# One VectorE transpose a level in a triangular inverse, the spreading and the constant terms given to other engines

## The chip, the cores and the metric

The kernel runs on one core of a Trainium2 chip. The core has five engines that run beside each other and wait for one another by semaphores: TensorE (PE, its weight loads PEld), VectorE (DVE), ScalarE (ACT), GpSimd (POOL) and SyncE (SP), whose queue issues the DMA transfers here. Each engine takes its own instructions in order. The metric is the device time of one execution in microseconds (us), lower is better; a kernel's time is the median of its runs.

## The reference

A two-layer trunk over 256 context and 1024 latent tokens of width 1024. In each layer a normalised and modulated input is projected once; half of the columns feed a retention group, the other half an RWKV-7 group of 8 heads of 64, in both directions of time. The part that matters here is the RWKV-7 scan, a generalised delta rule over a state of 64x64 a head:

```
S_t = S_{t-1} diag(w_t) - (S_{t-1} kap_t)(kap_t*a_t)^T + v_t k_t^T
y_t = S_t r_t
decay = exp(-exp(-softplus(-(w0 + tanh(xw) @ w2)) - 0.5))
```

With `decay = exp(-exp(-0.5) * sigmoid(z))` and `sigmoid(z) = 0.5*(1 + tanh(z/2))`, the product of decays over a stretch of tokens is an exponential of a running sum of `1 + tanh`.

## The kernel before

The scan is done in chunks of 64 tokens. A stage is one head pair (128 channels, two heads), two chunks, both directions: 10 stages a head pair, 4 head pairs a layer, 2 layers, so 80 stages. Three functions make a stage.

`prep` (L893 to L932) loads the features of a stage into `ft` (single-buffered), sums `1 + tanh` over each chunk of 64 with four VectorE scans (L908, L909; the `+ 1` of the first channel set, index 0, is the `ones` operand of the scan), takes the exponentials `em` and `ep` of the sums with their borders (L913, L914), and builds the scaled operands `own` and `bk`.

`prep2` (L934 to L1029) makes the products `gq` of these and then inverts a 64x64 unit triangular matrix for each chunk, direction and head. The two heads lie on the diagonal blocks of 128x128 fp16 tiles: `hi` is the matrix in fp16 (VectorE, L959), `lo` what fp16 leaves out (GpSimd, L963, L964). The inverse is made in six levels n = 0 to 5, each doubling the block size. A level is: four products with `hi` on TensorE (L980), a masked copy out of PSUM on VectorE (`xx`, L991), four products with the transposed inverse so far, `ttb` (L993), a copy out of PSUM on ScalarE (`tz`, L994), and the transpose of `tz` spread on the diagonal blocks of the next `ttb`. The spread is two VectorE transposes of 64 partitions at n = 1 to 3 (L973); at n = 4 one VectorE transpose of 128 partitions into `tt` (L1000) and two ScalarE copies (L973 too). At n = 0 the first `ttb` is a product of `hi` with a mask on VectorE (L987). Then two refinement steps: the residual `e` is identity minus product (VectorE, L1019), and `z1`, `z2` are product plus `tt` (VectorE, L1024, L1028). Two inverses run at a time, one in each of two PSUM banks and sets of buffers (`LANES = 2`).

`seq` advances the state from chunk to chunk with products of 64 columns and copies on ScalarE and VectorE.

All else (projections in three fp16 products each, L477 to L479, whose weights are split by ScalarE and GpSimd, L309 to L311; gates, retention, the output projection) is cut in small steps and handed out between the stages by `pump`, with a quota a stage (15 and 12 to 13). `seq` and `prep2` are given a higher priority. The order of each engine's instructions is made by the framework's scheduler from a model of times.

Of the kernel before, what the change touches and what calls it, by code (L numbers as in the profile page):

```python
# [47 lines left out]
BKB = 1  # L48
CSB = 1
ZB = 2  # L50
# [13 lines left out]
def shape_constants():  # L64
# [20 lines left out]
    bo[64:, 64:] = 1.0  # L85
    c["c_bo"] = bo
    j = np.arange(128, dtype=np.float32)
    rel = j[None, :] - j[:, None]
# [33 lines left out]
def hybrid_kernel(ctx: ExitStack, tc: tile.TileContext, a: dict, out: bass.AP, dbg: dict | None = None):  # L122
# [58 lines left out]
    load(bones32, a["c_bo"])  # L181
    kdix = cload("c_kd", [128, 4])
    id16 = const.tile([128, 64], F16, name="id16")
    lvm = const.tile([128, 2, 6, 64], F16, name="lvm")
    nc.vector.tensor_copy(id16[0:64], ident[0:64, 0:64])
    nc.vector.tensor_copy(id16[64:128], ident[64:128, 64:128])
    mhalf = const.tile([128, 1], F32, name="mhalf")
    nc.vector.memset(mhalf, -0.5)
    ones = const.tile([128, 64], F32, name="ones")
    nc.vector.memset(ones, 1.0)  # L190
    rowf = const.tile([128, 1], F32, name="rowf")
# [11 lines left out]
    def make_rings(sp):  # L203
        def ringof(nm, n, shape, dt):
            ring[nm] = [sp.tile(shape, dt, name=f"{nm}{k}") for k in range(n)]
            at[nm] = 0
            for t in ring[nm]:
                nc.gpsimd.memset(t, 0.0)

        ringof("cs", CSB, [128, 2, 2, 66], F32)  # L210
        ringof("hi", LANES, [128, 2, 2, 128], F16)
        ringof("lo", LANES, [128, 2, 2, 128], F16)
        ringof("eb", 1, [128, 2, 2, 128], F16)
        for k in range(LANES):
            ringof(f"ttb{k}", 2, [128, 2, 2, 128], F16)
        at["lane"] = 0

    def turn(key):
        at[key] += 1
        return ring[key][(at[key] - 1) % len(ring[key])]  # L220
# [144 lines left out]
    for l in range(DEPTH):  # L365
# [321 lines left out]
        def zstage(p):  # L687
# [9 lines left out]
            for t0, t1, _, _ in CONV:  # L697
                la = tz("lap")
                load(la, la_d[:, :, t0:t1].rearrange("i p t -> p i t"))
                for i in range(2):  # L700
# [9 lines left out]
                    for d in range(2):  # L710
                        nc.scalar.activation(th[:, d], pz[:, 256 * d:256 * d + 256], AF.Tanh,
                                             bias=(ha0 if i else hw0)(d, p), scale=0.5 / WS)
                    if i == 1:
                        nc.vector.tensor_scalar(th, th, 1.0, None, ALU.add)
                    load(feat_d[p][i:7 - i:6 - 2 * i, :, t0:t1].rearrange("d p t -> p d t"), th)
# [177 lines left out]
        def prep(sp, p, s):  # L893
# [5 lines left out]
            for i in range(2):  # L899
                for d in range(2):  # L900
# [4 lines left out]
                                     for j0, st in ((0, 9), (1, 7), (2, 3), (3, 3), (4, 3))]  # L905
            cs = turn("cs")
# [3 lines left out]
            ep = sp.tile([128, 2, 2, 66], F32, tag="ep", name="ep", bufs=1)  # L910
            em = sp.tile([128, 2, 2, 66], F32, tag="em", name="em", bufs=1)
            flat = lambda t: t.rearrange("p i d t -> p (i d t)")
# [21 lines left out]
        def prep2(sp, c):  # L934
# [22 lines left out]
            idb = ident[0:64, 0:64].unsqueeze(1).unsqueeze(1).to_broadcast([64, 2, 2, 64])  # L957
            for h in range(2):
                nc.vector.tensor_tensor(hi[HR[h], :, :, 64 * h:64 * h + 64], gq[0:64, h, :, :, 0:64], idb, ALU.add)  # L959
            il = sp.tile([128, 2, 2, 64], F32, tag="il", name="il", bufs=1)  # L960
            for h in range(2):
                cols = slice(64 * h, 64 * h + 64)
                nc.gpsimd.tensor_tensor(il[HR[h]], gq[0:64, h, :, :, 0:64], idb, ALU.add)  # L963
                nc.gpsimd.tensor_tensor(lo[HR[h], :, :, cols], il[HR[h]], hi[HR[h], :, :, cols], ALU.subtract)  # L964
            lane = at["lane"] = (at["lane"] + 1) % LANES
# [4 lines left out]

            def spread(dst, src, eng):
                for h in range(2):
                    eng(idr(dst[HR[h], :, :, 64 * h:64 * h + 64]), idr(src[HR[h]]))  # L973


            tz = ttb = tt = None
            for n in range(6):
# [4 lines left out]
                if n == 0:  # L982
                    nc.vector.tensor_tensor(tzn, q, mk, ALU.mult)  # L983
                    ttn = turn(f"ttb{lane}")
                    for d in range(2):
                        mt = lvm[:, 1 - d, 0, :].unsqueeze(1).unsqueeze(1).to_broadcast([128, 2, 2, 64])
                        nc.vector.tensor_tensor(ttn[:, :, d, :].rearrange("p i (h t) -> p i h t", h=2),  # L987
                                                hi[:, :, d, :].rearrange("p i (h t) -> p i h t", h=2), mt, ALU.mult)
                else:
                    xx = sp.tile([128, 2, 2, 64], F16, tag=f"xx{lane}", name="xx", bufs=1)  # L990
# [17 lines left out]
                tz, ttb = tzn, ttn  # L1008
            first = None
            for w in (hi, lo):  # L1010
                for i, d in ID:
                    tm = nc.tensor.matmul(q[:, i, d, :], w[:, i, d, :], tz[:, i, d, :], start=first is None, stop=w is lo,
                                          skip_group_check=True)
                    if first is not None:
                        behind(tm, first)
                    first = first or tm
# [4 lines left out]
            for i, d in ID:  # L1021
                nc.tensor.matmul(q[:, i, d, :], e[:, i, d, :], tt[:, i, d, :], start=True, stop=True)
            z1 = sp.tile([128, 2, 2, 64], F16, tag="z1", name="z1", bufs=1)
            nc.vector.tensor_tensor(z1, q, tt, ALU.add)  # L1024
            for i, d in ID:
                nc.tensor.matmul(q[:, i, d, :], e[:, i, d, :], z1[:, i, d, :], start=True, stop=True)
# [267 lines left out]
```

## Time and profile before

| | |
|---|---|
| median of 3 runs | 2549.21 us (2542.31 to 2556.64) |
| the profiled execution | 2541.74 us |
| its span, first to last instruction | 2540.0 us |
| mean granted TensorE clock | 0.945 |

Before 190 us the inputs are normalised and the first features made; layer 0's scan runs from about 190 to 1250 us, layer 1's from about 1430 to 2480 us. Busy time of TensorE is the union of its matmuls from issue to modelled end, so that matmuls overlap in it; in the other engines it is the time in which an instruction executes. Granted clock 1.0 is TensorE's upper level, 0.5 its lower one.

### The profile page before, as it was taken

What the parts mean: (1) busy time and instruction counts of PE and PEld (TensorE: products, weight loads), DVE (VectorE), ACT (ScalarE), POOL (GpSimd) and SP (SyncE); (2) the same over time, 40 slices, a digit from 0 to 9 for tenths busy, and PEclk for the clock granted to TensorE, in tenths of its full rate; (3) what the DMA queues carried; (4) which work ended last, traced back from release to release, by engine and by line L of the source; (5) the groups of instructions that cost most, each with busy time, mean ns of one, the idle gap of its engine ahead of it and who ended that gap; (6) DMA issues with size and microseconds to landing.
All of it is one profiled execution on the core that took longest, in us unless ns stands there. A gap on an engine that the chain in (4) does not pass through costs nothing. (4 is left out here: it accounts for less than half of the span.)

```text
span 2540.0 us, 68274 instructions
## 1 busy us (share of the span) xinstructions
PE 2332.3 (92%) x25223; PEld 1750.5 (69%) x25223; DVE 2016.9 (79%) x5822; ACT 1209.1 (48%) x3621; POOL 1017.3 (40%) x1511
## 2 busy tenths in 40 slices
PE   5789999999999999999986898999999999998997
PEld 2367767886787676777655677678768767676754
DVE  2658987998888787898657688889979988779866
ACT  4454554455455443345446545545645544334443
POOL 1444443344433433344425344444443444343442
PEclk8889999999999999799988899999999999987998
DMA  8754342444333432235433543434434433323444
GB/s 315 278 173 109 103 117 78 112 110 121 80 111 107 111 86 74 75 107 162 139 120 94 153 115 101 111 97 121 118 93 109 116 109 86 88 73 102 128 132 130
DMA packets 540013, 302.82 MB, mean 119 GB/s; under 512 B 239026, under 2 KB 526880, under 8 KB 537632
## 3 DMA queue, kind: packets, MB, share of 16 engines
q1 hardware_dynamic: 539680, 298.46, 41.0%
q8 instruction: 199, 3.26, 0.5%
q14 instruction: 134, 1.10, 0.1%
HBM read 212.21 MB, written 86.11 MB: 117 GB/s over the span
## 5 line engine op out<-in xcount | busy, mean ns | idle before, releaser
L477 PE MATMUL pproj<-h_hi,whi 128*128 128x256 f16 (+2 forms) x2128 | 632.2, 299 | 8.3 <-ACT h_hi L355 2.8
L478 PE MATMUL pproj<-h_lo,whi 128*128 128x256 f16 (+2 forms) x2128 | 632.3, 298 | 8.1 <-DVE h_lo L356 6.9
L479 PE MATMUL pproj<-h_hi,wlo 128*128 128x256 f16 (+2 forms) x2128 | 630.5, 298 | 4.5 <-POOL wlo L311 4.4
L311 POOL TENSOR_TENSOR wlo<-wraw,whi 128x256 f16<-128x256 f32 x360 | 252.2, 713 | 275.8 <-ACT wraw L310 230.9
L479 PEld LDWEIGHTS <-wlo 128*128 128x128 f16 x2128 | 214.0, 101 | 84.1 <-issue 13.1
L477 PEld LDWEIGHTS <-whi 128*128 128x128 f16 x2128 | 214.4, 101 | 74.3 <-issue 10.9
L478 PEld LDWEIGHTS <-whi 128*128 128x128 f16 x2128 | 213.3, 100 | 75.7 <-issue 16.1
L973 DVE STREAM_TRANSPOSE ttb<-tz 64x256 f16<-64x256 f16 x480 | 208.7, 435 | 29.2 <-ACT tz L994 24.4
L994 ACT CAST tz<-pinv 128x256 f16<-128x256 f32 x400 | 144.5, 370 | 178.1 <-PE pinv L993 161.6
L946 PE MATMUL pm<-own,bk 64*128 64x128 f32 (+1 forms) x1280 | 211.7, 300 | 9.5 <-DVE gq L949 4.6
L309 ACT ACTIVATE whi<-wraw 128x256 f16<-128x256 f32 x360 | 138.4, 412 | 153.9 <-DMA wraw<-in_w_in_dram 51.0
L963 POOL TENSOR_TENSOR il<-gq,c_id 64x256 f32<-64x256 f32 x160 | 122.9, 768 | 201.4 <-DVE gq L949 194.2
L946 PEld LDWEIGHTS pm<-own,bk 64*128 64x128 f32 x1280 | 168.9, 197 | 36.0 <-issue 10.9
L991 DVE TENSOR_TENSOR xx<-pinv,lvm 128x256 f16<-128x256 f32 x400 | 163.2, 416 | 36.0 <-PE pinv L980 32.7
L1049 PE MATMUL pseq<-st,own 64*64 64x64 f32 x2432 | 154.7, 231 | 0.0
L964 POOL TENSOR_TENSOR lo<-il,hi 64x256 f16<-64x256 f32 x160 | 116.9, 731 | 86.5 <-DVE hi L959 71.4
L310 ACT ACTIVATE wraw<-wraw 128x256 f32<-128x256 f32 x376 | 144.8, 410 | 4.4 <-ACT sbp L584 0.3
L980 PEld LDWEIGHTS <-hi 128*128 128x128 f16 x1920 | 105.1, 100 | 44.6 <-issue 17.3
L949 DVE TENSOR_TENSOR gq<-pm,c_m 128x256 f32<-128x256 f32 (+1 forms) x320 | 115.3, 400 | 25.0 <-PE pm L946 24.2
L1063 POOL TENSOR_TENSOR sf<-st,f 128x128 f32<-128x128 f32 x152 | 66.4, 437 | 164.7 <-DVE st L1081 147.9
L993 PE MATMUL pinv<-xx,ttb 128*128 128x64 f16 x1600 | 113.7, 196 | 16.6 <-DVE xx L991 15.4
L980 PE MATMUL pinv<-tz,hi 128*128 128x64 f16 x1600 | 115.6, 197 | 12.2 <-DVE tz L983 6.0
(250 smaller groups left out, 5648.9 us busy)
## 6 DMA issues: line engine op xcount, KB each, us to landing
ft<-feat SPq DMA_DIRECT2D x320, 160.0 KB
wraw<-in_w_in_dram SPq DMA_DIRECT2D x264, 128.0 KB
feat<-zth SPq DMA_DIRECT2D x80, 256.0 KB
wm<-in_w_mod_dram SPq DMA_DIRECT2D x16, 1024.0 KB
wraw<-in_w_out_dram SPq DMA_DIRECT2D x112, 128.0 KB
lap<-la SPq DMA_DIRECT2D x40, 256.0 KB
uv<-vt SPq DMA_DIRECT2D x320, 32.0 KB
wm<-in_w_mod_dram SPq DMA_DIRECT2D x16, 512.0 KB
```

Source lines behind the costliest of these rows:

```text
L309: nc.scalar.activation(hi, raw, AF.Copy, scale=WS)
L310: nc.scalar.activation(raw, raw, AF.Copy, scale=WS)
L311: nc.gpsimd.tensor_tensor(lo, raw, hi, ALU.subtract)
L477: nc.tensor.matmul(p[:, 0:n], hi[:, k, :], h_hi[:, kk, m0:m1], start=first, stop=False)
L478: nc.tensor.matmul(p[:, 0:n], hi[:, k, :], h_lo[:, kk, m0:m1], start=False, stop=False)
L479: nc.tensor.matmul(p[:, 0:n], lo[:, k, :], h_hi[:, kk, m0:m1], start=False, stop=stop)
L946: nc.tensor.matmul(pm[h][:, i, d, 0:q1], bk[HR[h], i, d, :], own[HR[h], i, d, 0:q1], start=True, stop=True)
L973: eng(idr(dst[HR[h], :, :, 64 * h:64 * h + 64]), idr(src[HR[h]]))
L980: nc.tensor.matmul(q[:, i, d, :], hi[:, i, d, :], id16 if n == 0 else tz[:, i, d, :], start=True, stop=True)
L991: nc.vector.tensor_tensor(xx, q, mk, ALU.mult)
L994: nc.scalar.copy(tzn, tp)
L1049: rm = nc.tensor.matmul(pq[HR[h], k, d, :], lhs, rhs, start=False, stop=stop, skip_group_check=True)
```

## The change

`prep`: the `+ 1` of index 0 is made once, where the features are made, by a GpSimd instruction of 128x512 (before, only index 1 had it there, on VectorE). One scan for each direction then runs over both chunks, 128 tokens, multiplying the running sum with `keep`, a constant from a new input that is 0 at the boundary of the chunks; two scans a stage and not four. `em` and `ep` become fixed tiles whose borders hold 1.0 from the start, and only their inner 64 columns are written.

`prep2`: `hi` is now a ScalarE copy of GpSimd's `il`. The first `ttb` is made by GpSimd. At n = 1 to 4 there is one VectorE transpose of 128 partitions into `tt`, and its two halves are copied to the diagonal blocks of `ttb`, one by ScalarE and one by GpSimd. The identity in `e` and the `tt` in `z1` and `z2` are added in PSUM by one more product each, 128x256, with a negated or plain 128x128 identity as weights; `e`, `z1` and `z2` are then plain ScalarE copies. Lane counts, priorities and quotas stay.

```diff
+    rs = np.ones((128, 2, 2, 64), np.float32)
+    rs[:, 0, :, 63] = 0.0
+    rs[:, 1, :, 0] = 0.0
+    c["c_rs"] = rs.reshape(128, 256)
...
+    keep = cload("c_rs", [128, 256])
+    one16 = const.tile([128, 128], F16, name="one16")
+    neg16 = const.tile([128, 128], F16, name="neg16")
+    nc.vector.tensor_copy(one16, ident)
+    nc.vector.tensor_scalar(neg16, ident, -1.0, None, ALU.mult)
...
-        ringof("cs", CSB, [128, 2, 2, 66], F32)
+        for nm in ("ep", "em"):
+            ringof(nm, 1, [128, 2, 2, 66], F32, 1.0)
...
-                    if i == 1:
-                        nc.vector.tensor_scalar(th, th, 1.0, None, ALU.add)
+                    (nc.vector if i else nc.gpsimd).tensor_scalar(th, th, 1.0, None, ALU.add)
                     load(feat_d[p][i:7 - i:6 - 2 * i, :, t0:t1].rearrange("d p t -> p d t"), th)
...
-            for i in range(2):
-                nc.vector.tensor_tensor_scan(cs[:, i, 0, 64:0:-1], ones[:, 0:64], twt[:, i, 0, ::-1], 0.0, ALU.add, ALU.add)
-                nc.vector.tensor_tensor_scan(cs[:, i, 1, 1:65], ones[:, 0:64], twt[:, i, 1, :], 0.0, ALU.add, ALU.add)
-            nc.scalar.activation(flat(em), flat(cs), AF.Exp, scale=-C2)
-            nc.scalar.activation(flat(ep), flat(cs), AF.Exp, scale=C2)
+            cs = sp.tile([128, 2, 128], F32, tag="cs", name="cs", bufs=1)
+            for d, (j, w) in enumerate(((0, slice(None, None, -1)), (9, slice(None)))):
+                nc.vector.tensor_tensor_scan(cs[:, d, w], keep[:, 128 * d:128 * d + 128][:, w],
+                                             ft[:, j].rearrange("p i t -> p (i t)")[:, w], 0.0, ALU.mult, ALU.add)
+            ep, em = turn("ep"), turn("em")
+            csv = cs.rearrange("p d (i t) -> p i d t", i=2)
+            nc.scalar.activation(em[:, :, :, 1:65], csv, AF.Exp, scale=-C2)
+            nc.scalar.activation(ep[:, :, :, 1:65], csv, AF.Exp, scale=C2)
...
-            for h in range(2):
-                nc.vector.tensor_tensor(hi[HR[h], :, :, 64 * h:64 * h + 64], gq[0:64, h, :, :, 0:64], idb, ALU.add)
             for h in range(2):
                 nc.gpsimd.tensor_tensor(il[HR[h]], gq[0:64, h, :, :, 0:64], idb, ALU.add)
+                nc.scalar.copy(hi[HR[h], :, :, 64 * h:64 * h + 64], il[HR[h]])
...
+            def spread(dst, src):
+                for h, eng in enumerate((nc.scalar.copy, nc.gpsimd.tensor_copy)):
                     eng(idr(dst[HR[h], :, :, 64 * h:64 * h + 64]), idr(src[HR[h]]))
+            def one_sum(lhs, rhs, parts):
+                one = nc.tensor.matmul(pc[:, 0:256], lhs, rhs, start=True, stop=False, skip_group_check=True)
+                for n, (w, x) in enumerate(parts):
+                    for i, d in ID:
+                        behind(nc.tensor.matmul(q[:, i, d, :], w[:, i, d, :], x[:, i, d, :], start=False,
+                                                stop=n == len(parts) - 1, skip_group_check=True), one)
...
-                        nc.vector.tensor_tensor(ttn[:, :, d, :].rearrange("p i (h t) -> p i h t", h=2),
+                        nc.gpsimd.tensor_tensor(ttn[:, :, d, :].rearrange("p i (h t) -> p i h t", h=2),
                                                 hi[:, :, d, :].rearrange("p i (h t) -> p i h t", h=2), mt, ALU.mult)
...
-                    if n < 4:
-                        ttn = turn(f"ttb{lane}")
-                        spread(ttn, tzn, nc.vector.transpose)
-                    elif n == 4:
+                    if n < 5:
                         tt = sp.tile([128, 2, 2, 64], F16, tag=f"tt{lane}", name="tt", bufs=1)
                         nc.vector.transpose(idr(tt), idr(tzn))
                         ttn = turn(f"ttb{lane}")
-                        spread(ttn, tt, nc.scalar.copy)
+                        spread(ttn, tt)
...
+            one_sum(neg16, id16.unsqueeze(1).to_broadcast([128, 4, 64]), [(hi, tz), (lo, tz)])
             e = turn("eb")
             for h in range(2):
-                nc.vector.scalar_tensor_tensor(idr(e[HR[h], :, :, 64 * h:64 * h + 64]), idr(q[HR[h]]), -1.0,
-                                               id16[HR[h]].unsqueeze(1).to_broadcast([64, 4, 64]), ALU.mult, ALU.add)
+                nc.scalar.activation(idr(e[HR[h], :, :, 64 * h:64 * h + 64]), idr(q[HR[h]]), AF.Copy, scale=-1.0)
+            one_sum(one16, flat(tt), [(e, tt)])
-            nc.vector.tensor_tensor(z1, q, tt, ALU.add)
+            nc.scalar.copy(z1, q)
+            one_sum(one16, flat(tt), [(e, z1)])
-            nc.vector.tensor_tensor(z2, q, tt, ALU.add)
+            nc.scalar.copy(z2, q)
```

## Rows read from the trace of the kernel before

**Rows 1.** The page's part 1: busy time, share of the span, instructions.
```profile
PE 2332.3 (92%) x25223; PEld 1750.5 (69%) x25223; DVE 2016.9 (79%) x5822; ACT 1209.1 (48%) x3621; POOL 1017.3 (40%) x1511
```

**Rows 2.** Windows: stretch, length, busy PE PEld DVE ACT POOL, PEclk, DMA.
```profile
190.00:1000.00 810.00, 782.05 (x8946) 604.44 (x8943) 683.13 (x2010) 393.88 (x1189) 326.18 (x480) 0.99 0.37 102
1000.00:1100.00 100.00, 94.74 (x955) 74.88 (x952) 83.67 (x258) 36.73 (x111) 40.70 (x60) 0.80 0.32 84
1100.00:1250.00 150.00, 136.95 (x1633) 105.83 (x1632) 126.16 (x375) 74.26 (x237) 68.96 (x106) 0.97 0.52 149
...
1430.00:1520.00 90.00, 80.40 (x805) 65.46 (x805) 77.53 (x202) 48.56 (x137) 35.20 (x54) 0.87 0.47 130
1520.00:2230.00 710.00, 684.84 (x7876) 520.75 (x7874) 606.39 (x1817) 348.63 (x1067) 294.19 (x438) 0.99 0.37 103
2230.00:2400.00 170.00, 151.96 (x1674) 120.74 (x1671) 148.87 (x445) 74.88 (x240) 68.69 (x105) 0.82 0.39 103
```

**Rows 3.** Timeline of PE near 1203 us: start, us, instruction.
```profile
1203.42 0.27 PE L806 MATMUL pout<-mh,wlo 128*128 128x256 f16 x1
1203.53 0.27 PE L804 MATMUL pout<-mh,whi 128*128 128x256 f16 x1
```

**Rows 4.** Groups by line and form, DVE: busy us, mean ns | idle before.
```profile
L973 DVE STREAM_TRANSPOSE ttb<-tz 64x256 f16<-64x256 f16 x480 | 208.7, 435 | 29.2 <-ACT tz L994 24.4
...
L959 DVE TENSOR_TENSOR hi<-gq,c_id 64x256 f16<-64x256 f32 x160 | 83.9, 524 | 7.9 <-PE pinv L1012 5.2
...
L1019 DVE SCALAR_TENSOR_TENSOR eb<-pinv,id 64x256 f16<-64x256 f32 x160 | 67.0, 418 | 4.9 <-PE pinv L1012 2.8
...
L908 DVE TENSOR_TENSOR_SCAN cs<-ones,ft 128x64 f32<-128x64 f32 x160 | 57.7, 360 | 52.5 <-DMA ft<-feat 51.7
...
L987 DVE TENSOR_TENSOR ttb<-hi,lvm 128x256 f16<-128x256 f16 x160 | 56.0, 389 | 0.6
L909 DVE TENSOR_TENSOR_SCAN cs<-ones,ft 128x64 f32<-128x64 f32 x160 | 55.4, 346 | 16.0 <-DMA ft<-feat 15.1
...
L1000 DVE STREAM_TRANSPOSE tt<-tz 128x256 f16<-128x256 f16 x80 | 34.7, 434 | 13.7 <-ACT tz L994 13.5
...
L1024 DVE TENSOR_TENSOR z<-pinv,tt 128x256 f16<-128x256 f32 x80 | 33.3, 416 | 10.5 <-PE pinv L1022 10.1
```

**Rows 5.** The same groups, ACT.
```profile
L994 ACT CAST tz<-pinv 128x256 f16<-128x256 f32 x400 | 144.5, 370 | 178.1 <-PE pinv L993 161.6 <-issue 5.7 <-DVE gq L949 2.9
L973 ACT COPY ttb<-tt 64x256 f16<-64x256 f16 x160 | 64.3, 402 | 45.7 <-DVE tt L1000 44.3
L794 ACT CAST mh<-mraw 128x256 f16<-128x256 f32 x69 | 26.9, 404 | 29.7 <-DMA mraw<-mix 29.4
```

**Rows 6.** The same groups, POOL.
```profile
L311 POOL TENSOR_TENSOR wlo<-wraw,whi 128x256 f16<-128x256 f32 x360 | 252.2, 713 | 275.8 <-ACT wraw L310 230.9 <-issue 9.7 <-PE pout L806 4.9
L963 POOL TENSOR_TENSOR il<-gq,c_id 64x256 f32<-64x256 f32 x160 | 122.9, 768 | 201.4 <-DVE gq L949 194.2 <-DMA lap<-la 2.0 <-PE pinv L980 1.2
L964 POOL TENSOR_TENSOR lo<-il,hi 64x256 f16<-64x256 f32 x160 | 116.9, 731 | 86.5 <-DVE hi L959 71.4 <-PE pseq L1049 3.2 <-PE pm L946 1.8
...
L919 POOL COPY f<-em 128x4 f32<-128x4 f32 x80 | 17.2, 215 | 65.2 <-ACT em L913 58.5 <-DMA wraw<-in_w_in_dram 2.8 <-DMA bon<-pvc 2.1
...
L346 POOL TENSOR_SCALAR ntm<-ntm,modA,modB 128x512 f32<-128x512 f32 x6 | 8.7, 1450 | 0.3
...
L208 POOL MEMSET ttb<- 128x512 f16 x8 | 3.9, 521 | 0.0
```

**Rows 7.** The instructions of L987: duration in ns, least, median and most.
```profile
L987 DVE TENSOR_TENSOR ttb<-hi,lvm x160: 244/283/817, 186.0 to 2424.1; 128x256 f16<-128x256 f16 x160
```

**Rows 8.** Groups by line and form, PE: idle before and what ended it.
```profile
L993 PE MATMUL pinv<-xx,ttb 128*128 128x64 f16 x1600 | 113.7, 196 | 16.6 <-DVE xx L991 15.4 <-ACT ttb L973 0.3 <-DVE kkd L574 0.2
```

**Rows 9.** Waits of SP's queue: waited for, us in total, times, longest.
```profile
SPq L323 <- POOL wlo L311: 190.1, 164, 11.7
```

More of the change, by code (lines that the diff above doesn't have):

```diff
@@ L48 @@
 BKB = 1
-CSB = 1
 ZB = 2
@@ L188, in hybrid_kernel @@
     nc.vector.memset(mhalf, -0.5)
-    ones = const.tile([128, 64], F32, name="ones")
-    nc.vector.memset(ones, 1.0)
     rowf = const.tile([128, 1], F32, name="rowf")
@@ L203, in make_rings, with ringof @@
     def make_rings(sp):
-        def ringof(nm, n, shape, dt):
+        def ringof(nm, n, shape, dt, value=0.0):
             ring[nm] = [sp.tile(shape, dt, name=f"{nm}{k}") for k in range(n)]
@@ L207, in ringof @@
             for t in ring[nm]:
-                nc.gpsimd.memset(t, 0.0)
-        ringof("cs", CSB, [128, 2, 2, 66], F32)
+                nc.gpsimd.memset(t, value)
+        for nm in ("ep", "em"):
+            ringof(nm, 1, [128, 2, 2, 66], F32, 1.0)
         ringof("hi", LANES, [128, 2, 2, 128], F16)
@@ L905, in prep @@
                                      for j0, st in ((0, 9), (1, 7), (2, 3), (3, 3), (4, 3))]
-            cs = turn("cs")
-            for i in range(2):
-                nc.vector.tensor_tensor_scan(cs[:, i, 0, 64:0:-1], ones[:, 0:64], twt[:, i, 0, ::-1], 0.0, ALU.add, ALU.add)
-                nc.vector.tensor_tensor_scan(cs[:, i, 1, 1:65], ones[:, 0:64], twt[:, i, 1, :], 0.0, ALU.add, ALU.add)
-            ep = sp.tile([128, 2, 2, 66], F32, tag="ep", name="ep", bufs=1)
-            em = sp.tile([128, 2, 2, 66], F32, tag="em", name="em", bufs=1)
-            flat = lambda t: t.rearrange("p i d t -> p (i d t)")
-            nc.scalar.activation(flat(em), flat(cs), AF.Exp, scale=-C2)
-            nc.scalar.activation(flat(ep), flat(cs), AF.Exp, scale=C2)
+            cs = sp.tile([128, 2, 128], F32, tag="cs", name="cs", bufs=1)
[6 more added lines that the diff above has]
+            nc.scalar.activation(ep[:, :, :, 1:65], csv, AF.Exp, scale=C2)
             two = lambda t: t.rearrange("p i d t -> p i (d t)")
@@ L957, in prep2 @@
             idb = ident[0:64, 0:64].unsqueeze(1).unsqueeze(1).to_broadcast([64, 2, 2, 64])
-            for h in range(2):
-                nc.vector.tensor_tensor(hi[HR[h], :, :, 64 * h:64 * h + 64], gq[0:64, h, :, :, 0:64], idb, ALU.add)
             il = sp.tile([128, 2, 2, 64], F32, tag="il", name="il", bufs=1)
             for h in range(2):
-                cols = slice(64 * h, 64 * h + 64)
                 nc.gpsimd.tensor_tensor(il[HR[h]], gq[0:64, h, :, :, 0:64], idb, ALU.add)
-                nc.gpsimd.tensor_tensor(lo[HR[h], :, :, cols], il[HR[h]], hi[HR[h], :, :, cols], ALU.subtract)
+                nc.scalar.copy(hi[HR[h], :, :, 64 * h:64 * h + 64], il[HR[h]])
             lane = at["lane"] = (at["lane"] + 1) % LANES
@@ L969, in prep2 @@
             idr = lambda t: t.rearrange("p i d t -> p (i d) t")
-            def spread(dst, src, eng):
-                for h in range(2):
+            def spread(dst, src):
+                for h, eng in enumerate((nc.scalar.copy, nc.gpsimd.tensor_copy)):
                     eng(idr(dst[HR[h], :, :, 64 * h:64 * h + 64]), idr(src[HR[h]]))
+            def one_sum(lhs, rhs, parts):
[4 more added lines that the diff above has]
+                                                stop=n == len(parts) - 1, skip_group_check=True), one)
             tz = ttb = tt = None
@@ L986, in prep2 @@
                         mt = lvm[:, 1 - d, 0, :].unsqueeze(1).unsqueeze(1).to_broadcast([128, 2, 2, 64])
-                        nc.vector.tensor_tensor(ttn[:, :, d, :].rearrange("p i (h t) -> p i h t", h=2),
+                        nc.gpsimd.tensor_tensor(ttn[:, :, d, :].rearrange("p i (h t) -> p i h t", h=2),
                                                 hi[:, :, d, :].rearrange("p i (h t) -> p i h t", h=2), mt, ALU.mult)
+                    for h in range(2):
+                        cols = slice(64 * h, 64 * h + 64)
+                        nc.gpsimd.tensor_tensor(lo[HR[h], :, :, cols], il[HR[h]], hi[HR[h], :, :, cols], ALU.subtract)
                 else:
@@ L1008, in prep2 @@
                 tz, ttb = tzn, ttn
[L1009 to L1016, printed above, removed]
+            one_sum(neg16, id16.unsqueeze(1).to_broadcast([128, 4, 64]), [(hi, tz), (lo, tz)])
             e = turn("eb")
             for h in range(2):
-                nc.vector.scalar_tensor_tensor(idr(e[HR[h], :, :, 64 * h:64 * h + 64]), idr(q[HR[h]]), -1.0,
-                                               id16[HR[h]].unsqueeze(1).to_broadcast([64, 4, 64]), ALU.mult, ALU.add)
-            for i, d in ID:
-                nc.tensor.matmul(q[:, i, d, :], e[:, i, d, :], tt[:, i, d, :], start=True, stop=True)
+                nc.scalar.activation(idr(e[HR[h], :, :, 64 * h:64 * h + 64]), idr(q[HR[h]]), AF.Copy, scale=-1.0)
+            flat = lambda t: t.rearrange("p i d t -> p (i d t)")
+            one_sum(one16, flat(tt), [(e, tt)])
             z1 = sp.tile([128, 2, 2, 64], F16, tag="z1", name="z1", bufs=1)
-            nc.vector.tensor_tensor(z1, q, tt, ALU.add)
-            for i, d in ID:
-                nc.tensor.matmul(q[:, i, d, :], e[:, i, d, :], z1[:, i, d, :], start=True, stop=True)
+            nc.scalar.copy(z1, q)
+            one_sum(one16, flat(tt), [(e, z1)])
             z2 = sp.tile([128, 2, 2, 64], F32, tag="z2", name="z2", bufs=ZB)
-            nc.vector.tensor_tensor(z2, q, tt, ALU.add)
+            nc.scalar.copy(z2, q)
             c.update(gq=gq, bt=bt, z2=z2)
```

## The prediction, made before the changed kernel ran

> **What bounds the kernel now.** I read the page's busy shares first. TensorE shows 92%, VectorE 79%, ScalarE 48%, GpSimd 40% [rows 1]. Shares over the whole span mix stages, and a matmul's modelled end overlaps the next one's start, so I went to the windows for where TensorE really stands idle, and to the timeline for what a product costs when it does not.
>
> In the two long stretches of the scans TensorE idles 810 - 782.1 = 28.0 us and 710 - 684.8 = 25.2 us, 3.5% of each, at a granted clock of 0.99 [rows 2]. There the projections that are handed out between the stages fill it: back to back, a product of 128x256 starts 0.11 us after the one before [rows 3]. The stretch 1100 to 1250 idles 13.1 us. I call these three the filled stretches: 66 us of idle in all.
>
> Three shorter ones look different: 1000 to 1100, 1430 to 1520 and 2230 to 2400 [rows 2]. VectorE is busy 83.7 + 77.5 + 148.9 = 310 of 360 us (86%), TensorE idles 5.3 + 9.6 + 18.0 = 33 us, and its granted clock is 0.80, 0.87 and 0.82. Full speed lost to the clock is 0.20 x 100 + 0.13 x 90 + 0.18 x 170 = 62 us. Here VectorE leads: the fill is thin and the stages themselves set the pace.
>
> So the bound is TensorE in the filled stretches, with VectorE close behind, and VectorE in the short ones. Before 190 us, between the scans and at the end, the change does next to nothing.
>
> A second reading matters for every latency below. Layer 0's scan, 190 to 1250 us [rows 2], holds 40 stages, 26.5 us each. With two lanes an inverse has 53 us. Its bare chain is short: a level is two products of about 0.2 us [rows 8], a masked copy of about 0.42 (as L1024), a copy of 0.37 and two transposes of 0.435 [rows 4, 5], some 2.1 us, so 12 or 13 us for six. The rest is queueing. Therefore I price engine time, and not the length of the chain.
>
> **The change, part by part.** VectorE, per kernel [rows 4]. Transposes: 480 of 0.435 us (208.7) become 240 of the L1000 kind, 240 x 0.434 = 104.2; it costs the same for 128 partitions as for 64; saved 104.5. `hi` leaves: 83.9. The first `ttb` leaves: 56.0. `e` leaves: 67.0. `z1` and `z2`, two groups of 80 like L1024: 160 x 0.416 = 66.6. Scans: 320 (57.7 + 55.4 = 113.1, mean 0.353) become 160 twice as long. No row has a scan of 128; it lies between 0.353 (all fixed cost) and 0.706 (all per element). I take the middle, 0.53, so 85; saved 28 (0 to 57). Together 406 us, 5.1 a stage: 2017 falls to 1611, 63% of the span.
>
> ScalarE gains [rows 5]: 320 half copies where 160 were, 160 x 0.402 = 64; `hi`, a conversion like L794, 160 x 0.404 = 65; `e`, `z1`, `z2` out of PSUM like L994, 320 x 0.370 = 118. That is 247 us, 3.1 a stage, to 1456 (57%). `em` and `ep` write 256 columns for 264: nothing.
>
> GpSimd gains [rows 6]: 320 half copies of 64x256 fp16. No row has that; 0.215 (128x4 copy) is below it, 0.731 (two inputs, same shape) above; the one-stream fp16 row, 0.521, is nearest, so 167 (69 to 234). The first `ttb`: 160 x 0.713 = 114. The `+ 1`: 40 between 0.521 and 1.450, I take 1.2, so 48 (21 to 58). Together 329 us (204 to 406), 4.1 a stage, to 1346 (53%). The transfer of `zth` on SP's queue then waits for GpSimd, and later loads of weights and of `ft` queue behind it; the features are made a head pair ahead, which hides it. Without that cover it costs up to 40 x 1.45 = 58 us of SP's time.
>
> TensorE gains three products of 128x256 a stage: 240 x 0.11 = 26 us [rows 3]. In the filled stretches nothing hides them. All other products stay.
>
> Latency: `hi` now comes after two `il` and a copy, 2 x 0.768 + 0.404 = 1.94 us and not 2 x 0.524 = 1.05 [rows 4 to 6]. The next `ttb` comes 0.434 + 0.52 = 0.95 us after `tz` and not 0.87, but VectorE is free for the masked copy 0.43 us sooner. The queueing above hides both; were the cover gone, 0.9 us a stage over two lanes is 36 us. At start one load of 128 KB, two small copies and a further memset come: under 2 us.
>
> One edit goes against a rule. The rows give the first `ttb` 0.389 us on VectorE [rows 4] and an instruction of its size 0.713 on GpSimd [rows 6]; in engine time the move loses 114 - 56 = 58 us. The Trainium skill, "GPSIMD Engine Reference", 4.1 Engine selection, says that elementwise work belongs on VectorE, since GpSimd takes about twice as long with two inputs; by that rule the sum would have 58 us of loss where mine has 56 of gain. The ratio here, 1.8, agrees with it. I keep the gain, since GpSimd is the emptiest engine [rows 1]. L987 also shows 0.283 in the median but up to 0.817 [rows 7], so something stretches such VectorE instructions; a busier GpSimd may stretch those that stay.
>
> The sum. In the short stretches there are 360 / 26.5 = 13.6 stages; VectorE's relief is worth at most 13.6 x 5.1 = 69 us there, and TensorE's idle plus clock, 33 + 62, allows it. I take half, 35, because ScalarE and GpSimd take up a part of the pace. In the filled stretches I take 20 of the 66 us of idle, since the waits there have many authors. Products cost 26. So -35 - 20 + 26 = -29 us: 2541.7 becomes 2513. The profiled execution ran 7.5 us below the median; on the median's scale the forecast is 2520 us (own range 2490 to 2540).
>
> **The rivals.** *TensorE has room* (larger gain). VectorE's whole relief arrives, the products fall into idle time: -69 - 66 = -135, 2414 us; half of it beyond my forecast, about 2465. For it: weight loads take only 69% of the span [rows 1]. Against it: starts 0.11 us apart leave no room between products [rows 3]. The Trainium skill, "Perfetto Trace Analysis", Identifying the Most-Contended Engine, tells to judge TensorE by weight-load share and not by matmul share; by that rule VectorE is the most contended engine here and this case follows.
>
> *Nothing comes back.* The waits in the filled stretches pass to other releasers, and VectorE's relief in the short ones is lost to the chain of `seq`; then TensorE's 26 us stand alone: 2549 to 2575. For it: 96.5% busy at full clock. Against it: the short stretches, where VectorE plainly leads.
>
> *GpSimd is late* (slower). Four half spreads and a first `ttb` a stage, 400 hand-overs, now stand in GpSimd's queue, and TensorE waits in order for `ttb` (L993) with all projections behind it. At 53% load a hand-over finds on average 0.53 x 0.72 / 2 = 0.19 us of another instruction in front: 76 us, or 38 if half hides behind the masked copy. Then 2549 - 55 + 26 + 38 to 76 = 2558 to 2596. It decides from 29 / 400 = 0.07 us a hand-over. For it: GpSimd's weight split stands 230.9 us in wait for ScalarE [rows 6], with a spread stuck behind it; and SP's weight loads already wait 190.1 us for that split [rows 9]. Against it: at n = 4 the kernel already spreads from one transpose by two copies, in series and in another engine's queue, and TensorE waited 0.3 us for these in all [rows 8].
>
> **How the numbers follow.** Forecast 0.45, TensorE has room 0.15, nothing comes back 0.20, GpSimd late 0.20. A measurement tells about 0.5% from no change, 2536 to 2562. Faster: 0.41 of the forecast and 0.15, so 0.56. Same: 0.04 of the forecast, 0.13 of nothing, 0.05 of GpSimd late: 0.22. Slower: the rest, 0.22. The range reaches from 2450, which leaves out the lower half of the larger gain, to 2585, which leaves out the upper part of the late GpSimd.
>
> **What would show it.** Right: VectorE's busy time near 1610, ScalarE's near 1455, GpSimd's near 1345; scans between 0.35 and 0.71 us; the three added products 0.11 us apart; the short stretches shorter with a granted clock above 0.9; the long ones about as long. Wrong: waits of L993's products for a GpSimd `ttb` over some 30 us; idle of TensorE in the filled stretches above 66 us; weight loads that land later because GpSimd's split is late; or VectorE's remaining instructions stretched so that less than 300 us go.

## The result, and the profile after

The changed kernel takes 2485.24 us (2482.61 to 2487.7, four runs) against 2548.59 us of the kernel before (four runs): a ratio of 0.9753, interval 0.9731 to 0.9776, so 63 us or 2.5% faster. The profiled execution took 2486.75 us, with a span of 2484.9 us and a mean granted clock of 0.956; it is 55 us shorter than the profiled execution before, against which the prediction's sum was made.

Part 1 of the page of the changed kernel answers to [rows 1].
```profile
PE 2319.4 (93%) x25463; PEld 1747.9 (70%) x25463; DVE 1715.6 (69%) x4783; ACT 1413.1 (57%) x4261; POOL 1327.8 (53%) x2033
```
VectorE lost 301 us of busy time, ScalarE gained 204, GpSimd 310. TensorE's busy time fell by 13 us although it has 240 products more. Its idle time fell from 2540.0 - 2332.3 = 207.7 us to 2484.9 - 2319.4 = 165.5. So the 55 us are 42 of idle and 13 of busy time. The first masked copy `xx` of layer 1 starts at 1410.0 us where it started at 1433.8: 24 of the 55 us lie before it and 31 behind.

The windows of the changed kernel, cut at about the same places of the program, answer to [rows 2] (stretch, length, busy PE PEld DVE ACT POOL, PEclk, DMA).
```profile
190.00:1000.00 810.00, 792.04 (x9294) 618.95 (x9293) 586.28 (x1683) 476.59 (x1447) 450.00 (x693) 0.99 0.38 105
1000.00:1100.00 100.00, 94.34 (x970) 71.20 (x969) 71.41 (x210) 47.38 (x145) 49.35 (x76) 0.90 0.33 86
1100.00:1235.00 135.00, 126.59 (x1457) 98.80 (x1456) 92.58 (x263) 79.78 (x253) 77.06 (x121) 0.97 0.55 159
...
1413.00:1500.00 87.00, 77.45 (x855) 64.86 (x852) 60.33 (x152) 56.20 (x162) 51.47 (x80) 0.93 0.47 130
1500.00:2205.00 705.00, 693.65 (x8110) 532.80 (x8111) 525.29 (x1517) 423.78 (x1302) 409.56 (x630) 0.99 0.39 106
2205.00:2350.00 145.00, 138.84 (x1683) 109.90 (x1680) 109.05 (x322) 85.61 (x279) 82.05 (x134) 0.95 0.40 106
```
In the filled stretches TensorE's idle time fell from 66 to 18.0 + 8.4 + 11.4 = 38 us. In the short ones it fell from 33 to 5.7 + 9.6 + 6.2 = 21, and the clock rose from 0.80, 0.87 and 0.82 to 0.90, 0.93 and 0.95: what it loses fell from 62 to 0.10 x 100 + 0.07 x 87 + 0.05 x 145 = 23 us. So the filled stretches gave back 28 us and the short ones up to 12 + 39 = 51. This is TensorE's own account: it holds the time that the 240 added products filled (26 us at 0.11 each), so it is not the worth of VectorE's relief. VectorE's share in the short stretches went from 86% to 241 / 332 = 73%.

The groups by line and form of the changed kernel: busy us, mean ns, idle before. They answer to [rows 4, 6, 8].
```profile
L1011 DVE STREAM_TRANSPOSE tt<-tz 128x256 f16<-128x256 f16 x320 | 139.1, 437 | 69.9 <-ACT tz L1008 62.2 <-POOL lo L1002 2.1 <-POOL il L966 1.2
L915 DVE TENSOR_TENSOR_SCAN cs<-c_rs,ft 128x128 f32<-128x128 f32 x160 | 79.5, 502 | 52.2 <-DMA ft<-feat 50.5
...
L976 POOL COPY ttb<-tt 64x256 f16<-64x256 f16 x320 | 140.8, 442 | 204.9 <-DVE tt L1011 172.9 <-PE pseq L1051 5.2 <-PE pout L812 3.7
L998 POOL TENSOR_TENSOR ttb<-hi,lvm 128x256 f16<-128x256 f16 x160 | 114.5, 734 | 17.2 <-ACT hi L967 16.3
L721 POOL TENSOR_SCALAR zth<-zth 128x512 f32<-128x512 f32 x40 | 62.3, 1558 | 16.6 <-ACT zth L719 8.6 <-DMA mraw<-mix 3.8 <-DMA ft<-feat 3.0
...
L1007 PE MATMUL pinv<-xx,ttb 128*128 128x64 f16 x1600 | 113.5, 195 | 5.5 <-DVE xx L1005 4.2 <-POOL ttb L976 0.8 <-DVE rst L647 0.2
```
The last row is the one to compare with [rows 8]: the products of a level waited 16.6 us before and wait 5.5 now. What fell is the wait for VectorE's masked copy `xx`, 15.4 to 4.2 us; the wait for GpSimd's half of `ttb` is 0.8 us in 1600 products.

### The profile page after: what moved, and what is told of

Read it like the earlier page. It is cut to its first block, busy times and chain, and to the rows that moved or that the text cites. A ratio compares the mean times of both kernels' runs of the same rounds, so it can differ in the third digit from the quotient of the medians.

```text
span 2484.9 us, 69488 instructions
## 1 busy us (share of the span) xinstructions
PE 2319.4 (93%) x25463; PEld 1747.9 (70%) x25463; DVE 1715.6 (69%) x4783; ACT 1413.1 (57%) x4261; POOL 1327.8 (53%) x2033
## 5 line engine op out<-in xcount | busy, mean ns | idle before, releaser
L976 POOL COPY ttb<-tt 64x256 f16<-64x256 f16 x320 | 140.8, 442 | 204.9 <-DVE tt L1011 172.9
L952 PE MATMUL pm<-own,bk 64*128 64x128 f32 (+1 forms) x1280 | 203.9, 296 | 9.6 <-DVE bk L935 4.9
L976 ACT COPY ttb<-tt 64x256 f16<-64x256 f16 x320 | 128.5, 402 | 107.6 <-DVE tt L1011 104.5
L1011 DVE STREAM_TRANSPOSE tt<-tz 128x256 f16<-128x256 f16 x320 | 139.1, 437 | 69.9 <-ACT tz L1008 62.2
L1002 POOL TENSOR_TENSOR lo<-il,hi 64x256 f16<-64x256 f32 x160 | 111.8, 699 | 40.8 <-ACT hi L967 33.1
L998 POOL TENSOR_TENSOR ttb<-hi,lvm 128x256 f16<-128x256 f16 x160 | 114.5, 734 | 17.2 <-ACT hi L967 16.3
```

Source lines behind the costliest of these rows:

```text
L952: nc.tensor.matmul(pm[h][:, i, d, 0:q1], bk[HR[h], i, d, :], own[HR[h], i, d, 0:q1], start=True, stop=True)
```

## The experiments

All ratios are to the kernel before, on the same chip. "us" is (ratio - 1) x 2548.59.

| kernel | what it is | ratio, interval | us |
|---|---|---|---|
| a_spread | before, with one transpose a level and the split spread | 0.9908, 0.9886 to 0.9929 | -23 |
| a_const | before, with the three products and ScalarE copies | 0.9919, 0.9891 to 0.9946 | -21 |
| a_scan | before, with the scans over both chunks | 0.9916, 0.9897 to 0.9935 | -21 |
| a_hi | before, with `hi` by ScalarE, first `ttb` by GpSimd | 0.9886, 0.9858 to 0.9915 | -29 |
| c_prod | before, and three idle products a stage | 1.0014, 0.9997 to 1.0031 | +4 |
| c_null | before, four products in another order | 1.0008, 0.9993 to 1.0024 | +2 |
| b_twice | changed, added products issued twice | 0.9728, 0.9707 to 0.975 | -69 |
| b_five | changed, added products issued five times | 1.0046, 1.0031 to 1.0062 | +12 |
| b_null | changed, four products in another order | 0.9752, 0.9735 to 0.9769 | -63 |
| b_dve | changed, and 960 idle VectorE transposes | 0.991, 0.9883 to 0.9936 | -23 |
| b_act | changed, both halves of the spread by ScalarE | 0.9767, 0.975 to 0.9784 | -59 |
| f_chain | changed, one more ScalarE copy in each level | 0.9754, 0.973 to 0.9777 | -63 |
| e_nospread | changed, spread as before | 0.9925, 0.9899 to 0.9951 | -19 |
| e_noconst | changed, constant terms as before | 0.9886, 0.9863 to 0.9908 | -29 |
| e_noscan | changed, scans as before | 0.9845, 0.982 to 0.9869 | -40 |
| e_nohi | changed, `hi` and first `ttb` as before | 0.9755, 0.9732 to 0.9779 | -62 |
| e_quota | before, with a smaller quota of handed-out steps | 0.9908, 0.9888 to 0.9928 | -23 |
| d_quota | changed, with the smaller quota | 0.968, 0.9654 to 0.9706 | -82 |

**Each part alone.** The kernel before with one part of the change; the lines that mark each part, in the order of the table:
```diff
-                        spread(ttn, tzn, nc.vector.transpose)
...
+                    if n < 5:
...
+                        spread(ttn, tt)
...
-            nc.vector.tensor_tensor(z2, q, tt, ALU.add)
+            one_sum(one16, flat(tt), [(e, z1)])
+            nc.scalar.copy(z2, q)
...
-                nc.vector.tensor_tensor_scan(cs[:, i, 1, 1:65], ones[:, 0:64], twt[:, i, 1, :], 0.0, ALU.add, ALU.add)
+                nc.vector.tensor_tensor_scan(cs[:, d, w], keep[:, 128 * d:128 * d + 128][:, w],
...
-                nc.vector.tensor_tensor(hi[HR[h], :, :, 64 * h:64 * h + 64], gq[0:64, h, :, :, 0:64], idb, ALU.add)
+                nc.scalar.copy(hi[HR[h], :, :, 64 * h:64 * h + 64], il[HR[h]])
```


> The kernel before with one part alone: one transpose of 128 partitions a level, spread by a ScalarE and a GpSimd copy. It frees 104 us of VectorE. Theory 1 (VectorE's time counts): the full change gave 63 us net of 26 us of added products, so 89 us for 406 us freed, 0.22 us for each; here 23 us faster, about 2526. Theory 2 (the length of a level's chain counts): this part holds nearly the whole gain, 50 us or more, below 2500. Theory 3 (GpSimd is late): slower than 2549.

> The kernel before with one part alone: identity and tt added in PSUM by a product each, e, z1 and z2 copied by ScalarE. It frees 134 us of VectorE and adds 240 products of 128x256. Theory 1: 29 us of gain less 26 us of products, within 0.3% of before. Theory 2: no shorter chain, so the products alone, 26 us slower, 2575. A third, TensorE has room for the products: 29 us faster, 2520.

> The kernel before with one part alone: the + 1 made once by GpSimd, two scans of 128 a stage for four of 64, fixed border tiles for em and ep. It frees 34 us of VectorE. Theory 1: 7 us faster, hard to tell from before. Theory 2: nothing. GpSimd late: slower by some 10 us, since the features of a head pair wait for 62 us of GpSimd.

> The kernel before with one part alone: hi copied by ScalarE from GpSimd's il, the first ttb made by GpSimd, lo after it. It frees 140 us of VectorE, adds 64 to ScalarE and 114 to GpSimd, and makes the head of the chain 0.9 us longer. Theory 1: 31 us faster, about 2518. Theory 2: up to 36 us slower, about 2585. GpSimd late: slower too, with TensorE waiting for the first ttb.

Measured: 23, 21, 21 and 29 us, 94 in all, where the whole brings 63. Every part is worth something alone, a_const among them although it adds the 240 products that I charged with 26 us. `hi` gains most, by a margin within the intervals, although it moves the first `ttb` to an engine that takes 734 ns for what VectorE did in 389 [rows 4].

**What a product costs.** Idle products in the kernel before (with a kernel that only swaps the order of four products, for the size of an accident of order), and the added products issued more often in the changed one:
```diff
+                if n in (1, 2, 3):
+                    lv = lvm.rearrange("p d n t -> p (d n t)")
+                    nc.tensor.matmul(pc[:, 0:256], lv[:, 0:128], lv[:, 0:256], start=True, stop=True)
...
-            ID = [(i, d) for i in range(2) for d in range(2)]
+            ID = [(i, d) for d in range(2) for i in range(2)]
...
+                nc.tensor.matmul(pc[:, 0:256], lhs, rhs, start=True, stop=True)
```
The last line stands once in b_twice and four times in b_five.

> The kernel before with three products of 128x256 more in a stage, at levels 1 to 3, each overwritten by the products of its level: 240 in all, TensorE's part of the change by itself. The prediction's step (nothing hides them in the filled stretches): 26 us slower, ratio 1.010. The theory that doubling them in the changed kernel left (TensorE waits in its queue more than its busy share shows, and the products go into these waits): ratio 0.997 to 1.003.

> The kernel before with the four products of a level issued in another order (chunks inside directions), as in the same test of the changed kernel: no work added or taken. If each single part gained 10 us or so beyond its VectorE time because the order of before happens to be a poor one, this is 5 to 15 us faster as well, ratio 0.994 to 0.998. If the parts' gains are their own, it is within 0.2% of before.

> The changed kernel with each of the three added products of a stage issued twice (the first is overwritten by the second): 240 more products of 128x256 on TensorE and nothing else. TensorE bound as predicted: 26 us slower than the changed kernel, about 2511. TensorE has room: no slower than 2490. The constant terms alone made the kernel before faster, which leans to the second.

> The changed kernel with each added product issued five times (the last one counts): 960 products of 128x256 more, 960 x 0.11 = 105 us of TensorE. If waits take them up without end, within 10 us of the changed kernel, ratio near 0.975. If the room is the few tens of us that the doubling used, 60 to 105 us slower, ratio 1.00 to 1.016. I expect between these: 50 us slower, 0.995.

Part 1 of the pages of c_prod and then of b_five:
```profile
PE 2346.7 (92%) x25463; PEld 1770.5 (70%) x25463; DVE 2019.3 (79%) x5822; ACT 1207.7 (47%) x3621; POOL 1023.2 (40%) x1511
```
```profile
PE 2398.2 (94%) x26423; PEld 1829.3 (72%) x26423; DVE 1726.8 (68%) x4783; ACT 1418.8 (56%) x4261; POOL 1325.4 (52%) x2033
```
The 240 idle products cost 4 us (-1 to +8), and the order alone moves as much. In the profiled execution of c_prod (span 2543.5) TensorE is 14 us busier than in that of before and its idle time falls from 207.7 to 196.8. They stand in the levels and not in the refinement steps, where the change has its own. Windows of c_prod, cut as in [rows 2]:
```profile
190.00:1000.00 810.00, 786.55 (x9043) 610.54 (x9041) 685.48 (x2025) 389.96 (x1185) 332.27 (x483) 0.99 0.37 102
1000.00:1100.00 100.00, 91.97 (x984) 68.57 (x983) 81.67 (x251) 37.99 (x114) 37.97 (x55) 0.86 0.32 83
...
2230.00:2400.00 170.00, 154.70 (x1733) 124.92 (x1734) 150.04 (x443) 77.68 (x246) 73.57 (x112) 0.86 0.41 108
```
In the filled stretches the idle time falls from 66 to 23.5 + 9.7 + 22.7 = 56 us, in the short ones from 33 to 30. The granted clock of the short ones is 0.86, 0.94 and 0.86, where it was 0.80, 0.87 and 0.82 (and 0.80, 0.86 and 0.80 in c_null): what it loses falls from 62 to 43 us. From 1100 to 1250 us it is 0.91 for 0.97, 9 us lost. So the products went into waits and into stretches whose clock rose with them: 26 - 10 - 3 - 19 + 9 = 3 us, nearer to the measured 4 than single executions warrant.

240 more in the changed kernel cost nothing either. Room ends, though: from b_twice to b_five there are 720 products more, 79 us at 0.11 each, and the time rises by 0.0318 x 2548.59 = 81 us. Over these a product costs its whole price.

**Whose time it is.** Four kernels after the change: a swapped order; idle transposes of [128, 256] fp16 in `prep` ahead of `em`, which give VectorE back as much time as it lost; no GpSimd in the spread; and a longer chain.
```diff
-            ID = [(i, d) for i in range(2) for d in range(2)]
+            ID = [(i, d) for d in range(2) for i in range(2)]
...
+            for k in range(12):
+                nc.vector.transpose(idle16.rearrange("p (n t) -> p n t", n=4), lvm[:, 0, 0:4, :])
...
-                for h, eng in enumerate((nc.scalar.copy, nc.gpsimd.tensor_copy)):
+                for h, eng in enumerate((nc.scalar.copy, nc.scalar.copy)):
...
-                    nc.scalar.copy(tzn, tp)
+                    nc.scalar.copy(hop, tp)
+                    nc.scalar.copy(tzn, hop)
```


> The changed kernel with the four products of a level, of each refinement step and of the residual issued in another order (chunks inside directions): the same instructions, lengths and waits. It shows how far the order that the scheduler makes moves the time by itself. All theories expect the changed kernel's 2485 us; whatever it differs by bounds what a single part's difference can tell. I expect less than 10 us.

> The changed kernel with 12 idle transposes of 128x256 on VectorE a stage, from a constant to a tile that nobody reads: 960 x 0.435 = 418 us of VectorE back, and no chain that depends on them. Theory 1 (VectorE's time counts): the whole gain and the products' price are lost, 2548 to 2575. Theory 2 (chain length): the time stays near 2485, at most 20 us above, as VectorE has idle time enough.

> The changed kernel with both halves of the spread copied by ScalarE, one after the other: 141 us off GpSimd, 129 us on ScalarE. If GpSimd's half spread costs the changed kernel time, this is 10 us or more faster, below 2475. If the halves are hidden behind the masked copy, it is within 10 us; if the level's chain counts, it is slower by 0.4 us at 4 levels of 40 stages in a lane, 64 us a layer at most.

> The changed kernel with one more ScalarE copy in every level of the inverse: the copy out of PSUM goes to a further tile, and from there a second one makes the tile that is transposed. It adds 400 x 0.37 = 148 us to ScalarE and 0.4 us to the chain of each level, and nothing to VectorE. Theory A, the chain of an inverse sets the pace: five levels of 0.4 us in 80 stages on two lanes are up to 80 us, ratio up to 1.007. Theory B, the chain waits in queues anyway: within 10 us of the changed kernel, ratio 0.972 to 0.979.

The idle transposes of b_dve (duration in ns, least, median and most; first and last start), a window of b_dve, and part 1 of the page of f_chain:
```profile
L919 DVE STREAM_TRANSPOSE idle<-lvm x960: 391/432/448, 86.4 to 1192.6; 128x256 f16<-128x256 f16 x192
```
```profile
190.00:1000.00 810.00, 773.42 (x8868) 604.22 (x8867) 772.17 (x2266) 456.77 (x1392) 425.90 (x659) 0.98 0.37 102
```
```profile
PE 2302.8 (94%) x25463; PEld 1744.0 (71%) x25463; DVE 1718.8 (70%) x4783; ACT 1537.3 (62%) x4661; POOL 1323.9 (54%) x2033
```
With VectorE as busy in all as before the change (2022.9 us), 40 of the 63 us are gone. But the load did not lie where it lay before. Nobody reads what the idle transposes write, and in the order that the scheduler made all 960 start before 1193 us: some 24 a stage of layer 0 and none in layer 1. VectorE is busy 95% of the window shown, 84% before the change and 72% after it. Of the 41 us between the profiled executions of b_dve and of the changed kernel, 38 lie ahead of layer 1's first masked copy (1447.6 and 1410.0 us) and 4 behind it. So a VectorE that is 95% busy costs time; that the load of the kernel before, spread as it was, is worth 40 us is not shown by this run.

With 124 us more on ScalarE and a copy more in every level nothing is lost, and with all of the spread on ScalarE nothing that can be told. So neither the length of the chain nor ScalarE's time is scarce here. That VectorE's is, rests on b_dve's layer 0 and on the parts taken one by one.

**One part undone.** The changed kernel with one part as before, so that the other three stand (edits as in the first group, turned round):
```diff
-                        spread(ttn, tt)
+                        spread(ttn, tzn, nc.vector.transpose)
...
-            nc.scalar.copy(z2, q)
+            nc.vector.tensor_tensor(z2, q, tt, ALU.add)
...
-                nc.vector.tensor_tensor_scan(cs[:, d, w], keep[:, 128 * d:128 * d + 128][:, w],
+                nc.vector.tensor_tensor_scan(cs[:, i, 1, 1:65], ones[:, 0:64], twt[:, i, 1, :], 0.0, ALU.add, ALU.add)
...
-                        nc.gpsimd.tensor_tensor(ttn[:, :, d, :].rearrange("p i (h t) -> p i h t", h=2),
+                        nc.vector.tensor_tensor(ttn[:, :, d, :].rearrange("p i (h t) -> p i h t", h=2),
```


> The changed kernel with the transposes and the spread as before (two VectorE transposes a level at n = 1 to 3, two ScalarE copies at n = 4); all else changed. VectorE gets 104 us back. Theory A, VectorE's time is the common currency and its value falls as more of it is free: a loss of 104 x 40/418 = 10 us against the changed kernel, so a ratio to before near 0.979. Theory B, each part keeps the gain it had alone except one that becomes redundant: a loss of 23 us, ratio 0.984. Theory C, a gain of the order of the instructions and not of VectorE's time: no relation to the 104 us.

> The changed kernel with the constant terms added by VectorE as before, without the three products. VectorE gets 134 us back, ScalarE loses 118. Theory A: a loss of 134 x 40/418 = 13 us, ratio near 0.980. Theory B: 21 us, ratio 0.984. By the price of my prediction (26 us for the products) it would be faster than the changed kernel by 13 us, ratio 0.970.

> The changed kernel with four scans a stage over 64 tokens each, the borders of the exponentials written in every stage and the addition on GpSimd left out, as before. VectorE gets some 34 us back. Theory A: a loss of 3 us, ratio near 0.9766. Theory B, with this part as the redundant one, since the wait of the scans for the features, which it took away when it was alone, is there again in the changed kernel: no loss, 0.975; if it keeps the gain that it had alone, a loss of 21 us, ratio 0.984.

> The changed kernel with the fp16 matrix and the first transposed operand made by VectorE as before, and GpSimd's remainder right behind each. VectorE gets 140 us back. Theory A: a loss of 140 x 40/418 = 13 us, ratio near 0.980. Theory B: 29 us, ratio 0.987.

Measured losses against the changed kernel: spread 0.0172 x 2548.59 = 44 us, constant terms 34, scans 23, `hi` 1. Both theories miss. A fails in order and size: the scans gave VectorE least and cost 23. B has the form right, one part redundant, but it is `hi` and not the scans, and the spread is worth twice what it gained alone. Part 1 of the pages of e_nospread, e_noconst and e_nohi:
```profile
PE 2329.7 (93%) x25463; PEld 1759.0 (70%) x25463; DVE 1822.2 (73%) x5024; ACT 1373.2 (55%) x4101; POOL 1185.3 (47%) x1713
```
```profile
PE 2321.2 (93%) x25223; PEld 1746.7 (70%) x25223; DVE 1824.1 (73%) x5102; ACT 1306.6 (52%) x3941; POOL 1319.7 (53%) x2033
```
```profile
PE 2314.4 (93%) x25463; PEld 1746.6 (70%) x25463; DVE 1806.6 (73%) x5104; ACT 1350.9 (54%) x4101; POOL 1232.7 (50%) x1873
```
VectorE's busy time is the same within 18 us in the three, and their times are 2523.59, 2510.34 and 2478.68 us. So it matters which of VectorE's instructions go, or what takes their place: the parts differ in the other engines too. The second products of a level differ between them; the group in e_nospread, in e_nohi and then in c_prod:
```profile
L1011 PE MATMUL pinv<-xx,ttb 128*128 128x64 f16 x1600 | 117.3, 196 | 17.1 <-DVE xx L1009 14.6 <-ACT ttb L979 2.2
```
```profile
L1011 PE MATMUL pinv<-xx,ttb 128*128 128x64 f16 x1600 | 116.9, 195 | 9.7 <-DVE xx L1009 7.7 <-ACT ttb L982 1.6
```
```profile
L996 PE MATMUL pinv<-xx,ttb 128*128 128x64 f16 x1600 | 114.2, 196 | 21.9 <-DVE xx L994 21.0
```
With two transposes a level the wait for `xx` is back at 14.6 us, where before it was 15.4 [rows 8] and after 4.2. This wait does not give the time, though: in c_prod it is 21.0 us with a time 4 us from that of before, and in b_dve 3.5 us with 40 us lost. Why the spread is worth 44 us and `hi` nothing is not shown.

**The fill.** The quota of handed-out steps, in the changed kernel and in the one before:
```diff
-QUOTA = ((15.0, 15.0), (12.0, 13.0))
+QUOTA = ((14.0, 15.0), (11.0, 13.0))
```


> The changed kernel with one microsecond less of fill a stage for the first three head pairs (quotas 14 and 11 for 15 and 12). If the short stretches lose time because the fill has run out before the last head pair, TensorE idles less there and the time falls by 5 to 25 us, ratio 0.965 to 0.973. If VectorE or the chain sets the pace everywhere, it stays at 0.975 or rises, as the fill is then late at the end of a layer.

> The kernel before with the quotas of handed-out steps at 14 and 15, and 11 and 13, in place of 15 and 15, and 12 and 13; all else as before. Theory A, the short stretches lose time because the fill has run out by then: the same quota that took some 18 us off the changed kernel takes 15 to 25 off this one, ratio 0.990 to 0.994. Theory B, VectorE leads there before the change, so that more fill would only wait with it: a ratio of 0.998 to 1.002.

The smaller quota takes 23 us off the kernel before and 19 off the changed one: two gains that add up. Where they come from was not settled. In the profiled execution of e_quota, 24 us shorter than that of before, layer 0's last masked copy starts at 1249.1 us (1296.1 before) and layer 1's first at 1419.3 (1433.8). In the 90 us from there, 1419 to 1509 and 1434 to 1524, TensorE starts 902 products where it started 830, at a clock of 0.91 for 0.89, with VectorE as busy (80.3 and 77.5 us). That is a little more work beside the same VectorE; in 1000 to 1100 the clock is 0.81, as good as before. So the fill runs in other places, and that the short stretches lacked it is not shown. The changed kernel with the smaller quota is the fastest of all, 2461.72 us.

## Why the prediction was right and wrong

**The direction was right; the gain was double the forecast.** -29 us were forecast on the profiled execution, -55 measured, and -63 by the medians. The time lies in the wide range and below the likeliest case's own.

**The step that failed** is "TensorE gains three products of 128x256 a stage ... In the filled stretches nothing hides them ... Products cost 26". They cost 4 us in the kernel before (c_prod), and a second 240 cost nothing in the changed one (b_twice). The 0.11 us of [rows 3] are right for back-to-back products, and they are the price from b_twice to b_five; the mistake was to take the filled stretches for back to back. Their 66 us of idle time stood in the same rows, and 26 fit: c_prod lost 10 us of idle there and 3 in the short ones, and got 19 back by the clock of the short ones, which my sum left out of the price. Without this term my sum is -35 - 20 = -55, which is what the two profiled executions differ by; the agreement is closer than the terms deserve.

**The two terms of relief**, 35 and 20, can't be read off one by one. The filled stretches gave back 28 us of idle and the short ones up to 51 of idle and clock, 79 in all; with the 26 us that the added products fill it is 79 - 26 = 53, near the 55 of my two terms. But c_prod, with no relief at all, gets 10 + 3 + 19 = 32 us of the same idle and clock back (and loses 9 by the clock of 1100 to 1250), so what VectorE's relief brought in either kind of stretch stays open. I halved the term of the short ones "because ScalarE and GpSimd take up a part of the pace"; in f_chain and b_act more work on ScalarE costs nothing, so for ScalarE the reason did not hold.

**The relief as a rate.** I summed 406 us of VectorE's instructions and let each of them count alike. Work on VectorE does cost time where it is 95% busy (b_dve). But spread, constant terms and scans make 62 us together (e_nohi) from singles of 23 + 21 + 21 = 65, and 140 us of my 406, `hi` and the first `ttb`, bring 29 us alone and nothing as the fourth. Why they don't add up was not settled. Of VectorE's busy time 301 us went and not 406: the instructions that went make 416 us (own sum), but those that stayed became 59 us longer, and what is left of the difference is overlap, which busy time counts once.

**The durations** were good. Scans of 128 took 0.502 us (I took 0.53), GpSimd's half copy 0.442 (0.52), its first `ttb` 0.734 (0.713); its `+ 1` took 1.56, above my upper end of 1.45.

**TensorE has room** was the rival nearest to what happened: by mechanism right, by its 2414 to 2465 us too far. The room is real and limited. The rule of the Trainium skill ("Perfetto Trace Analysis", Identifying the Most-Contended Engine), to judge TensorE by weight-load share and by its FLOPs against the peak, pointed to this side, and c_prod agrees: the share of weight loads goes from 69% to 70% and the time stays. But from b_twice to b_five, 71% to 72%, every product is paid for: 70% of weight loads was not 30% of room.

**Nothing comes back** fell by both of its halves: the waits in the filled stretches didn't pass to others, and the products had no price that could stand alone. **GpSimd is late** fell by L1007's 0.8 us of waiting for `ttb`, and b_act, with no GpSimd in the spread, is no faster. SP's loads of weights did wait longer for GpSimd's split, 216.6 us where it was 190.1 [rows 9], and that didn't show in the time.

**What stays open.** Which part of VectorE's relief brought the gain, and by what wait. Idle work on VectorE took back 40 us, but all of it in layer 0 at 95% busy; the same work held in every stage, or between the copies of a level where the removed instructions stood, wasn't tried. The chain is not the rest (f_chain), nor, as far as the quota's like gain before and after tells, the fill. The parts add up neither alone (94 us) nor undone (102).

## What to carry to other kernels

An engine at 96% busy by modelled ends may still take work for next to nothing (here 240 products in the kernel before and 240 more in the changed one, 26 us each at 0.11): before charging added work to it, issue it idle in the kernel as it is, and go on until it costs. Where a scheduler makes the order, read from the trace where idle work ran before concluding from it: here 960 transposes meant for 80 stages ran in 40. Do not price a relief by busy time: with VectorE equally busy within 18 us, undoing a part cost between nothing and 44 us. And undo each part in the finished kernel: the part that gained most alone gained nothing there.

## What the runs showed of the hardware

Two groups of VectorE instructions with two inputs in SBUF became longer when GpSimd had more to do. First as they are in the kernel before, then the same two after:
```profile
L926 DVE TENSOR_TENSOR bk<-ft,bk 128x256 f32<-128x256 f32 x80 | 39.6, 494 | 0.6
L929 DVE TENSOR_TENSOR bk<-bk,em 128x256 f32<-128x256 f32 x80 | 37.4, 467 | 3.3 <-POOL bk L928 3.2
```
```profile
L932 DVE TENSOR_TENSOR bk<-ft,bk 128x256 f32<-128x256 f32 x80 | 46.6, 583 | 0.8
L935 DVE TENSOR_TENSOR bk<-bk,em 128x256 f32<-128x256 f32 x80 | 43.0, 537 | 8.1 <-POOL bk L934 7.8
```
VectorE's instructions that both kernels have sum to 1672 us before and 1731 after (own sum of their durations); ScalarE's to 1297.1 and 1296.9. The Trainium skill ("GPSIMD Engine Reference", 1. Specifications) says that GpSimd shares its SBUF interfaces with VectorE and contends with VectorE instructions with two SBUF inputs; the rows agree in kind, and ScalarE's unchanged sum too. The size does not follow GpSimd's share of the span alone: the first of the two groups takes 659 ns in e_nospread, where GpSimd is busy 47%. What GpSimd runs beside the very instruction tells more (own count, by start and end in the traces). Those of the first group during which no GpSimd instruction ran took 415 ns in the mean before and 417 after, none over 427; there are 32 of them in 80 before and 10 after. The others took 547 and 607. In e_nospread it is 14 at 412 ns, and 711 for the others.
